# Attention mixer of a decoder trunk: layer norm and conv branch one head pair earlier, output tiles opened during the last scores

## The chip, the cores and the metric

The kernel runs on one core of a Trainium2 chip. The core has a matrix engine (PE; its weight loads are listed apart as PEld), a vector engine (DVE), a scalar engine for activation functions and copies (ACT), a general engine (POOL) and a queue engine (SP). Here POOL and SP are used mostly to start DMAs. Each engine works through its own list of instructions strictly in order, and a semaphore holds an instruction back until what it needs is there. The metric is the device time of one execution in microseconds (us), the median of several runs.

## What is computed

A trunk of two layers on 512 tokens of width 1024: a half-weighted SwiGLU block, a mixer, another half-weighted SwiGLU block, each on an RMS-normed input, and a last norm. The change is in the mixer of layer 0, which runs an attention branch and a convolution branch side by side:

```python
def hybrid_mixer(h, cos, sin, w_in, dw_w, dw_b, ln_g, ln_b, w_out):
    proj = h @ w_in
    q = apply_partial_rotary(heads(proj[..., :A_WIDTH]), cos, sin)
    k = apply_partial_rotary(heads(proj[..., A_WIDTH:2 * A_WIDTH]), cos, sin)
    v = heads(proj[..., 2 * A_WIDTH:3 * A_WIDTH])
    ...                      # three dilated windows of 8 heads, mixed by their softmax denominators
    u = proj[..., 3 * A_WIDTH:]
    glu = u[..., :CONV_CHANNELS] * jax.nn.sigmoid(u[..., CONV_CHANNELS:])
    c = causal_depthwise_conv(glu, dw_w) + dw_b
    c = jax.nn.silu(layer_norm(c, ln_g, ln_b))
    return jnp.concatenate([attn, c], axis=-1) @ w_out
```

The kernel folds the three windows into one softmax with an additive mask. All data are float32; a matrix product is made of three passes of the faster rounded format (high part by high part, low by high, high by low).

## The kernel before: how the mixer is staged

Data lie transposed: 128 channels on the partitions, 512 tokens along a row. The input of the output projection has eight chunks of 128 channels, `o_x[0..7]`. Chunks 0 to 3 are the four head pairs (two heads of 64 channels each), chunks 4 to 7 the four channel groups of the convolution branch. Each chunk is kept as a high part `hi` and a low part `lo`, made by `split` (ACT copy, L134, then DVE subtraction, L135).

`hybrid_heads` works head pair by head pair, `t` = 0 to 3:

- `raw_rows` projects q or k of a pair (24 matmuls, L140 to L142, of 128x512), and `rotate` applies the rotary part (a matmul with a permutation, L859; DVE L861, L862; then the high and low parts, ACT L864 and DVE L865, named `qh`, `ql`, `kh`, `kl`).
- `scores(t)` makes eight blocks of scores, four for each of the pair's two heads. A block is three matmuls (L880 to L882) of 128, 256, 384 or 512 columns into a PSUM tile named `sc`. DVE adds the mask and takes the row extreme (L885), ACT takes the exponential (L886). `normed` divides by the denominators (DVE L890, ACT L892).
- `values(t, b)` transposes a head's probabilities (ten transposes, L912), copies them out of PSUM (ACT L915, tiles `pt`) and multiplies by v (four float32 matmuls, L920) into a tile `po`. The values of pair t stand after the projections of pair t+1.

The convolution is a row of 31 DVE instructions per channel group (`taps`, L773 and L777). `layer_norm` is a Python generator in five steps, each started by a `next(ln)`: the sum over the four groups and the mean by a matmul (L925 to L928); subtraction of the mean, squares and their sum by matmuls (L932 to L941); the reciprocal root (L944 and `rsqrt`, ten small DVE instructions); its broadcast by matmuls (`row_bcast`, L156) and the multiplication (L951 to L953); Silu and `split` (L956, L957). In the kernel before, three of these steps stand before the scores of pair 3 and two behind them.

The output projection makes eight tiles d = 0 to 7 of 128 channels, each of 8 chunks times 3 matmuls (`out_mm`). Tiles 0 to 2 are begun in `hybrid_heads` with chunks 0, 1, 2 and completed in `hybrid` with chunks 4 to 7 and 3. Tiles 3 to 7 follow whole. The weights of one tile come in by `load_split`: a DMA from SP into a buffer `raw` (four buffers), an ACT copy into `whi` (L126), a second ACT copy with the sign turned into `wlo` (L127), and a DMA from POOL that adds the original onto it (L128). `whi` and `wlo` have three buffers each (`NWB`, L31), so the weights of tile 3 go into those of tile 0. `raw` of tile 3 is loaded long before.

PSUM has eight banks, in four groups of two: `mm`, `sc`, `po`, `tr`. The mean of the layer norm takes one of the two `sc` banks until the four subtractions L932 have read it. The order in which `hybrid` and `hybrid_heads` write their instructions is only a priority: a scheduler places them on the engines, and what it makes of them is read from the order of the built program.

Of the kernel before, what the change touches and what calls it, by code (L numbers as in the profile page):

```python
# [50 lines left out]
def trunk(ctx, tc, io, out, phases):  # L51
# [45 lines left out]
    def psum(tag):  # L97
        return pp.tile([P, T], F32, tag=tag, name=nm(tag))
# [614 lines left out]
    def hybrid(xn, nxt, ahead, take):  # L713
        with tc.tile_pool(name="ho", bufs=1, side="right", reuse_waits="tile") as op:
            with tc.tile_pool(name="hy", bufs=1, side="right", reuse_waits="tile") as hp:
                o_x, ps = hybrid_heads(xn, op, hp, take)
            xn.close()
            nxt.open()
            for d in range(NK):
                if d < 3:  # L720
                    out_mm(ps[d], take(20 + d), o_x, (4, 5, 6, 7, 3), False, True)
                else:
                    ps[d] = psum("po" if d % 2 else "mm")
                    wt = take(20 + d)
                    for _ in range((0, 0, 0, 0, 0, 0, 1, 1)[d]):
                        step(ahead)
                    out_mm(ps[d], wt, o_x, range(NK), True, True)
                V.tensor_add(h[d], ps[d], h[d])
                nxt.feed(d)
                for _ in range((0, 0, 0, 0, 0, 0, 2, 2)[d]):  # L730
                    step(ahead)
            nxt.fed()

    def out_mm(ps, wt, xs, ks, first, last):
        for k in ks:
            hi, lo = wt[k // 4]
            c = slice(k % 4 * P, k % 4 * P + P)
            mm3(ps, hi[:, c], lo[:, c], xs[k], first and k == ks[0], last and k == ks[-1])

    def hybrid_heads(xn, op, hp, take):  # L740
# [21 lines left out]
        pads, cv, o_x = [], [], [None] * NK  # L762
# [20 lines left out]
        def taps(n):  # L783
            for _ in range(n):
                next(conv, None)
# [61 lines left out]
        def raw_rows(i, n):  # L847
            ps = project(i)
            taps(n)
            qa = ht("qa", 2)  # L850
            A.activation(qa, ps, AF.Copy)
            u = ht("u", 2)
            V.tensor_mul(u, ps, Ct)
            return qa, u
# [10 lines left out]
            V.tensor_sub(lo, u, hi.bitcast(F32))  # L865
            return hi, lo

        def scores(t, q, k):
            qh, ql = q
            kh, kl = k  # L870
            probs = {}
            den = {b: ht("den", 4, n=4) for b in range(2)}
            rd = {b: ht("rd", 4, n=4) for b in range(2)}

            def score(b, i):
                rows = slice(64 * b, 64 * b + 64)
                w = (i + 1) * P
                c = slice(i * P, w)
                ps = psum("sc")
                PE.matmul(ps[:, :w], qh[rows, c], kh[rows, :w], start=True, stop=False)  # L880
                PE.matmul(ps[:, :w], qh[rows, c], kl[rows, :w], start=False, stop=False)
                PE.matmul(ps[:, :w], ql[rows, c], kh[rows, :w], start=False, stop=True)  # L882
                s = ht(f"s{i}", 2, n=w)
                m = ht("m", 8, n=1)
                V.tensor_tensor_reduce(s, ps[:, :w], K["mask"][:, T - w:], -0.125, 3.0e38, ALU.add, ALU.min, m)  # L885
                A.activation(s, s, AF.Exp, scale=-1.0, bias=m, accum_out=den[b][:, i:i + 1])  # L886
                probs[b, i] = s

            def normed(b):
                V.reciprocal(rd[b], den[b])  # L890
                for i in range(NT):
                    A.activation(probs[b, i], probs[b, i], AF.Copy, scale=rd[b][:, i:i + 1])  # L892

            for i in range(NT):
                score(0, i)
            score(1, 0)
            score(1, 1)
            normed(0)
            score(1, 2)
            score(1, 3)  # L900
            normed(1)
            return probs

# [18 lines left out]
        def layer_norm():  # L922
            mu = psum("sc")
            tot = ht("t1", 1)
            V.tensor_add(tot, cv[0], cv[1])  # L925
            V.tensor_add(tot, tot, cv[2])
            V.tensor_add(tot, tot, cv[3])
            PE.matmul(mu, K["o512"].to_broadcast([P, P]), tot, start=True, stop=True)  # L928
            yield
            acc = ht("t1", 1)  # L930
            for t in range(4):
                V.tensor_sub(cv[t], cv[t], mu)  # L932
                if t == 0:
                    A.activation(acc, cv[t], AF.Square)
                else:
                    sq = ht("qa", 2)
                    A.activation(sq, cv[t], AF.Square)
                    V.tensor_add(acc, acc, sq)
            st = psum("tr")
            for c in range(NT):  # L940
                PE.matmul(st[:, c:c + 1], acc[:, c * P:(c + 1) * P], K["o512"], start=True, stop=True)  # L941
            yield
            v = small(4, "nv")
            V.tensor_scalar(v, st[:, :4], EPS, None, op0=ALU.add)  # L944
            rl = rsqrt(v, 4, "rcol")
            yield
            rb = psum("tr")
            for c in range(NT):
                row_bcast(rl[:, c:c + 1], rb[:, c * P:(c + 1) * P])
            Rl = ht("t1", 1)  # L950
            A.activation(Rl, rb, AF.Copy)  # L951
            for t in range(4):
                V.tensor_mul(cv[t], cv[t], Rl)  # L953
            yield
            for t in range(4):
                A.activation(cv[t], cv[t], AF.Silu, scale=pr["lng"][:, t:t + 1], bias=pr["lnb"][:, t:t + 1])  # L956
                o_x[4 + t] = split(cv[t], op, "ox", 16)  # L957

        ln = layer_norm()
        q = raw_rows(12, 0)  # L960
        k = raw_rows(13, 4)
        qr = rotate(q, "q", 2)
        held = None
        out_ps = {}
        for t in range(NT):
            if t < 3:
                q = raw_rows(14 + 2 * t, 8)
            else:
                next(ln)
            kr = rotate(k, "k", 1)  # L970
            if held:
                values(t - 1, 0, *held)
            if t < 3:
                k = raw_rows(15 + 2 * t, 8)
                qn = rotate(q, "q", 2)
            else:
                next(ln)
            if held:
                values(t - 1, 1, *held)
                o_x[t - 1] = split(held[1], op, "ox", 16)  # L980
            if t == 3:
                next(ln)
            probs = scores(t, qr, kr)
            taps(5)
            qr = qn
            held = probs, psum("po")
        next(ln)
        for d in range(3):
            out_ps[d] = psum("sc" if d > 1 else "mm")
            out_mm(out_ps[d], take(20 + d, 3 - d), o_x, (0, 1, 2), True, False)  # L990
        next(ln, None)
        values(3, 0, *held)
        values(3, 1, *held)
        o_x[3] = split(held[1], op, "ox", 16)
# [458 lines left out]
```

## Time and profile before

| | |
|---|---|
| median of 3 runs | 2097.8 us (2097.16 to 2097.91) |
| the profiled execution | 2098.93 us, its span 2097.2 us |
| mean granted PE clock | 0.974 |
| busy share of the span | PE 96%, PEld 85%, DVE 77%, ACT 53%, POOL 6% |
| last output tile of the mixer complete (L728) | 621.98 us from the span's start |

Times within the profile are counted from the start of its span. A row of the timeline gives the start, the busy time, the engine, the line of the kernel and the operation, `output<-inputs` by the program's tile names with the buffer numbers left out, the shape, how many instructions were merged (x), and in square brackets how long the engine had been idle before and what ended that. A float32 matmul appears as two instructions. The busy time of a matmul covers its latency: what one costs in a row of others is the distance between two starts. PEclk is the granted clock as a share of the full one. In the table of windows, each engine has its busy time and the number of instructions in that stretch.

### The profile page before, as it was taken

What the parts mean: (1) busy time and instruction counts of PE and PEld (TensorE: products, weight loads), DVE (VectorE), ACT (ScalarE), POOL (GpSimd) and SP (SyncE); (2) the same over time, 40 slices, a digit from 0 to 9 for tenths busy, and PEclk for the clock granted to TensorE, in tenths of its full rate; (3) what the DMA queues carried; (4) which work ended last, traced back from release to release, by engine and by line L of the source; (5) the groups of instructions that cost most, each with busy time, mean ns of one, the idle gap of its engine ahead of it and who ended that gap; (6) DMA issues with size and microseconds to landing.
All of it is one profiled execution on the core that took longest, in us unless ns stands there. A gap on an engine that the chain in (4) does not pass through costs nothing.

```text
span 2097.2 us, 32970 instructions
## 1 busy us (share of the span) xinstructions
PE 2020.4 (96%) x12694; PEld 1785.7 (85%) x12694; DVE 1609.0 (77%) x2758; ACT 1113.9 (53%) x1981; POOL 134.0 (6%) x190
## 2 busy tenths in 40 slices
PE   7999999999999999998999999979989999999997
PEld 6999998786579999987999998767778878999986
DVE  5888879798567888889888788657585578888876
ACT  5444447547654444465444446676445654444455
POOL 0000000110000000000000000233302210000000
PEclk9999999999899999999999999999889999999998
DMA  3333332784143333322333332679635563333321
GB/s 125 101 103 109 101 100 83 183 194 97 29 101 116 101 104 108 96 86 84 107 104 105 101 101 82 183 215 231 137 106 131 121 132 107 109 101 102 104 87 46
DMA packets 108845, 237.70 MB, mean 113 GB/s; under 512 B 22160, under 2 KB 24976, under 8 KB 108688
## 3 DMA queue, kind: packets, MB, share of 16 engines
q1 hardware_dynamic: 90544, 193.06, 29.7%
q0 software_dynamic: 17616, 42.02, 10.8%
q8 instruction: 99, 1.62, 0.3%
q14 instruction: 58, 0.48, 0.1%
q10 hardware_dynamic: 528, 0.52, 0.1%
HBM read 224.55 MB, written 11.01 MB: 112 GB/s over the span
## 4 chain that ended last, share of the span: by engine, by line
PE 80%; DVE 8%; issue 5%; ACT 3%; DMA 3%; SPq 0%; POOL 0%; DVEq 0%; ACTq 0%; POOLq 0%
PE mm L141 13%; PE mm L140 13%; PE mm L142 13%; PE sc L141 7%; PE sc L140 7%; PE sc L142 7%; PE po L142 3%; PE po L141 2%; PE po L140 2%; PE tr L140 2%; PE tr L142 2%; PE tr L141 2%; DVE wlo L117 1%; DVE gl L386 1%; PE tr L1051 1%
## 5 line engine op out<-in xcount | busy, mean ns | idle before, releaser
L117 DVE TENSOR_TENSOR wlo<-raw,whi 128x1024 fp32r<-128x1024 f32 (+1 forms) x400 | 473.3, 1201 | 158.8 <-ACT whi L116 154.3
L140 PE MATMUL mm<-xh,whi 128*128 128x256 f32 (+2 forms) x1800 | 562.0, 312 | 8.7 <-ACT b L456 4.0
L142 PE MATMUL mm<-xh,wlo 128*128 128x256 f32 (+2 forms) x1800 | 557.9, 310 | 3.0 <-DMA wlo<-in_wgdn 3.0
L141 PE MATMUL mm<-xl,whi 128*128 128x256 f32 (+2 forms) x1800 | 556.3, 309 | 0.0
L116 ACT ACTIVATE whi<-raw 128x1024 fp32r<-128x1024 f32 (+1 forms) x400 | 404.8, 1034 | 33.9 <-issue 14.4
L140 PEld LDWEIGHTS mm<-xh,whi 128*128 128x128 f32 (+1 forms) x1800 | 344.7, 192 | 42.4 <-ACT b L456 7.2
L141 PEld LDWEIGHTS mm<-xl,whi 128*128 128x128 f32 (+1 forms) x1800 | 344.6, 191 | 26.3 <-issue 1.1
L142 PEld LDWEIGHTS mm<-xh,wlo 128*128 128x128 f32 (+1 forms) x1800 | 344.7, 192 | 20.5 <-DMA wlo<-in_wgdn 3.6
L140 PE MATMUL sc<-xh,whi 128*128 128x256 f32 x1056 | 299.8, 284 | 5.8 <-ACT xh L250 3.0
L141 PE MATMUL sc<-xl,whi 128*128 128x256 f32 x1056 | 299.0, 283 | 3.4 <-DVE xl L251 3.4
L142 PE MATMUL sc<-xh,wlo 128*128 128x256 f32 x1056 | 298.8, 283 | 0.9 <-DVE wlo L117 0.8
L140 PEld LDWEIGHTS sc<-xh,whi 128*128 128x128 f32 x1056 | 202.0, 191 | 7.8 <-ACT xh L250 3.6
L141 PEld LDWEIGHTS sc<-xl,whi 128*128 128x128 f32 x1056 | 202.1, 191 | 4.0 <-DVE xl L251 4.0
L142 PEld LDWEIGHTS sc<-xh,wlo 128*128 128x128 f32 x1056 | 202.1, 191 | 1.8 <-DVE wlo L117 1.8
L386 DVE TENSOR_TENSOR gl<-g,gh 128x512 fp32r<-128x512 f32 (+1 forms) x286 | 178.6, 643 | 32.3 <-ACT gh L385 30.0
L385 ACT ACTIVATE gh<-g 128x512 fp32r<-128x512 f32 (+1 forms) x286 | 166.4, 592 | 67.1 <-PE mm L141 34.8
L403 ACT ACTIVATE a<-a 128x512 f32<-128x512 f32 x88 | 55.6, 632 | 253.8 <-DVE a L402 253.8
L126 ACT ACTIVATE whi<-raw 128x512 fp32r<-128x512 f32 (+2 forms) x109 | 77.0, 734 | 97.9 <-PE mm L141 72.0
L442 ACT ACTIVATE b<-mm 128x256 f32<-128x256 f32 x84 | 32.2, 383 | 155.9 <-PE mm L142 155.9
L456 ACT ACTIVATE b<-mm 128x256 f32<-128x256 f32 x88 | 33.7, 383 | 141.0 <-PE mm L142 141.0
L141 PE MATMUL mm<-gl,whi 128*128 128x512 f32 (+1 forms) x220 | 83.1, 378 | 4.9 <-DVE gl L386 4.7
L777 DVE SCALAR_TENSOR_TENSOR cv<-pad,prm_t,cv 128x512 f32<-128x512 f32 x120 | 83.8, 743 | 0.8
(419 smaller groups left out, 3544.8 us busy)
## 6 DMA issues: line engine op xcount, KB each, us to landing
raw<-in_wf1i SPq DMA_DIRECT2D x82, 512.0 KB, 3.6
raw<-in_wf2i SPq DMA_DIRECT2D x82, 512.0 KB, 3.5
raw<-in_wgdn SPq DMA_DIRECT2D x32, 512.0 KB, 5.2
wlo<-in_wgdn POOLq DMA_DIRECT2D x64, 256.0 KB, 6.1
raw<-in_wf2i SPq DMA_DIRECT2D x56, 256.0 KB, 2.6
raw<-in_wf1i SPq DMA_DIRECT2D x52, 256.0 KB, 2.6
raw<-in_wf1b SPq DMA_DIRECT2D x20, 512.0 KB, 3.5
raw<-in_wf2b SPq DMA_DIRECT2D x20, 512.0 KB, 3.5
```

The source lines that it names most:

```text
L116: A.activation(hi[:, s], src[:, s], AF.Copy)
L117: V.tensor_sub(lo[:, s], src[:, s], hi[:, s].bitcast(F32))
L126: A.activation(hi[:, s], raw[:, s], AF.Copy)
L140: PE.matmul(ps, whi, xhi, start=first, stop=False, skip_group_check=skip)
L141: PE.matmul(ps, whi, xlo, start=False, stop=False, skip_group_check=skip)
L142: PE.matmul(ps, wlo, xhi, start=False, stop=last, skip_group_check=skip)
L385: A.activation(hi, g[f][:, s], AF.Copy)
L386: V.tensor_sub(lo, g[f][:, s], hi.bitcast(F32))
L403: A.activation(cg[f], cg[f], AF.Silu)
L442: A.activation(b0[f][:, HT:], pb[f][:, :HT], AF.Copy)
L456: A.activation(b1[f][:, :HT], pb[f][:, :HT], AF.Copy)
L777: V.scalar_tensor_tensor(acc, x, w, acc, op0=ALU.mult, op1=ALU.add)
```

## The change

Four things are written in another order; no arithmetic is changed, and no instruction is added to PE or DVE.

- The taps of the convolution are requested earlier: 10, 10 and 6 of them at each of pairs 0 and 1, then 8 and 3, in place of 8, 8 and 5 at every pair, so that none is left for pair 3.
- `layer_norm` begins one pair earlier: its first step stands before the scores of pair 2, the second behind them, the other three before the scores of pair 3.
- A generator `open_out` emits one piece behind each of the eight score blocks of pair 3: chunks 0, 1, then 4 to 7, then 2, for output tiles 0 and 1.
- Output tile 2 is emitted whole but for chunk 3 behind the scores. `hybrid` then adds only chunk 3 to tiles 0 to 2.

```diff
-                    out_mm(ps[d], take(20 + d), o_x, (4, 5, 6, 7, 3), False, True)
+                    out_mm(ps[d], take(20 + d), o_x, (3,), False, True)
...
-        def scores(t, q, k):
+        def scores(t, q, k, fill=lambda: None):
...
             for i in range(NT):
                 score(0, i)
+                fill()
             score(1, 0)
+            fill()
             score(1, 1)
+            fill()
             normed(0)
             score(1, 2)
+            fill()
             score(1, 3)
+            fill()
             normed(1)
...
+        def open_out():
+            for d, ks in ((0, (0, 1)), (1, (0, 1)), (0, (4, 5)), (1, (4, 5)), (0, (6, 7)), (1, (6, 7)),
+                          (0, (2,)), (1, (2,))):
+                if d not in out_ps:
+                    out_ps[d] = psum("mm")
+                out_mm(out_ps[d], take(20 + d, 3 - d), o_x, ks, ks[0] == 0, False)
+                yield
+
...
+        opening = open_out()
+        more = ((10, 10, 6), (10, 10, 6), (8, 3, 0))
         for t in range(NT):
             if t < 3:
-                q = raw_rows(14 + 2 * t, 8)
-            else:
+                q = raw_rows(14 + 2 * t, more[t][0])
+            kr = rotate(k, "k", 1)
+            if t == 3:
                 next(ln)
-            kr = rotate(k, "k", 1)
             if held:
                 values(t - 1, 0, *held)
             if t < 3:
-                k = raw_rows(15 + 2 * t, 8)
+                k = raw_rows(15 + 2 * t, more[t][1])
                 qn = rotate(q, "q", 2)
             else:
                 next(ln)
             if held:
                 values(t - 1, 1, *held)
                 o_x[t - 1] = split(held[1], op, "ox", 16)
+            if t == 2:
+                next(ln)
             if t == 3:
+                next(ln, None)
+            probs = scores(t, qr, kr, (lambda: next(opening, None)) if t == 3 else (lambda: None))
+            if t < 3:
+                taps(more[t][2])
+            if t == 2:
                 next(ln)
-            probs = scores(t, qr, kr)
-            taps(5)
             qr = qn
             held = probs, psum("po")
-        next(ln)
-        for d in range(3):
-            out_ps[d] = psum("sc" if d > 1 else "mm")
-            out_mm(out_ps[d], take(20 + d, 3 - d), o_x, (0, 1, 2), True, False)
-        next(ln, None)
+        out_ps[2] = psum("sc")
+        out_mm(out_ps[2], take(22, 1), o_x, (0, 1, 4, 5, 6, 7, 2), True, False)
         values(3, 0, *held)
         values(3, 1, *held)
         o_x[3] = split(held[1], op, "ox", 16)
```

What the scheduler makes of it, at three places. Lines behind the change are shifted: its L917, L925 and L933 are the L912, L920 and L928 of before. The first place is PE where the two programs part, while the values of pair 1 are still being made (`tr` and `po` tiles); before, the scores of pair 2 (`sc`) begin there:

```order
L880 MATMUL sc_5262<-kh_5151,qh_4987 128x128
L881 MATMUL sc_5262<-kl_5152,qh_4987 128x128
L912 MATMUL tr_5238<-cst,s_848_5066 128x128
L912 MATMUL tr_5238<-cst,s_851_5079 128x128
L912 MATMUL tr_5238<-cst,s_854_5087 128x128 x2
L882 MATMUL sc_5262<-kh_5151,ql_4988 128x128
```

With the change, output tiles 0 and 1 (`mm_5483`, `mm_5505`) are begun there with chunks 0 (`hi_5023`) and 1 (`hi_5258`, and `lo` beside them), and these rows lead up to the mean of the layer norm and the first score of pair 2:

```order
L140 MATMUL mm_5483<-hi_5258,whi_5114 128x512
L140 MATMUL mm_5505<-hi_5258,whi_5190 128x512
L141 MATMUL mm_5483<-lo_5259,whi_5114 128x512
L142 MATMUL mm_5483<-hi_5258,wlo_5115 128x512
L141 MATMUL mm_5505<-lo_5259,whi_5190 128x512
L933 MATMUL sc_5262<-t_892_5263,hcst 128x512
L880 MATMUL sc_5272<-kh_5161,qh_4996 128x128
L881 MATMUL sc_5272<-kl_5162,qh_4996 128x128
```

The pieces with chunks 0 and 1, written behind the scores of pair 3, have moved ahead of those of pair 2, and the scores of pair 2 stand behind the split of pair 1 and the mean. On PE and DVE every row ahead of this place is the same in both programs, the taps among them.

The second place is DVE between the last score block of pair 2 and the first of pair 3. Before, the low part of pair 3's k (`kl_5353`) came straight after the subtraction of the mean:

```order
L862 TENSOR_TENSOR u_5220<-u_5220,t_923_5349 128x512
L890 RECIPROCAL rd_5261<-den_5259 128x4
L932 TENSOR_TENSOR cv_4456<-cv_4456,sc_5341 128x512
L932 TENSOR_TENSOR cv_4702<-cv_4702,sc_5341 128x512
L932 TENSOR_TENSOR cv_4971<-cv_4971,sc_5341 128x512
L865 TENSOR_TENSOR kl_5353<-u_5220,kh_5352 128x512
```

With the change, it stands behind the last score block of pair 2 (`sc_5333`) and the small instructions of the reciprocal root:

```order
L885 ISA s_919_5337,m_5338<-sc_5333,hcst 128x512
L885 ISA m_5338 128x1
L862 TENSOR_TENSOR u_5224<-u_5224,t_928_5369 128x512
L150 TENSOR_TENSOR nt_5379<-rcol_5378 128x4
L151 SCALAR_TENSOR_TENSOR nt_5379<-nt_5379,nv_5376 128x4
L152 SCALAR_TENSOR_TENSOR rcol_5378<-nt_5379,rcol_5378 128x4
L150 TENSOR_TENSOR nt_5379<-rcol_5378 128x4
L151 SCALAR_TENSOR_TENSOR nt_5379<-nt_5379,nv_5376 128x4
L152 SCALAR_TENSOR_TENSOR rcol_5378<-nt_5379,rcol_5378 128x4
L150 TENSOR_TENSOR nt_5379<-rcol_5378 128x4
L890 RECIPROCAL rd_5271<-den_5269 128x4
...
L865 TENSOR_TENSOR kl_5373<-u_5224,kh_5372 128x512
```

The root has moved ahead of the scores of pair 3, and `kl`, for which those scores wait, behind most of it.

The third place is PE around the last values. Between the last score of pair 3 and the first transpose for its values, the change has 51 matmuls of output tiles 0 to 2 in one block, with no score among them. Then come the values, and these rows (`hi_5669` and `lo_5670` are chunk 3, the last one to be ready; `whi_5696` and `whi_5717` are the weights of tiles 3 and 4):

```order
L925 MATMUL po_5600<-pt_5658,vt_4583 64x128
L140 MATMUL mm_5483<-hi_5669,whi_5114 128x512
L140 MATMUL mm_5505<-hi_5669,whi_5190 128x512
L140 MATMUL sc_5601<-hi_5669,whi_5486 128x512
L141 MATMUL mm_5483<-lo_5670,whi_5114 128x512
L142 MATMUL mm_5483<-hi_5669,wlo_5115 128x512
L141 MATMUL mm_5505<-lo_5670,whi_5190 128x512
L142 MATMUL mm_5505<-hi_5669,wlo_5191 128x512
L141 MATMUL sc_5601<-lo_5670,whi_5486 128x512
L142 MATMUL sc_5601<-hi_5669,wlo_5487 128x512
L140 MATMUL po_5736<-hi_5023,whi_5696 128x512
L141 MATMUL po_5736<-lo_5024,whi_5696 128x512
```

Before, the same place had the rest of three tiles, 36 matmuls from the last of the values to the first of tile 3; it began so (`hi_5633` is chunk 3, `hi_5568` and `hi_5573` are chunks 4 and 5):

```order
L140 MATMUL mm_5530<-hi_5583,whi_5104 128x512
L141 MATMUL mm_5530<-lo_5584,whi_5104 128x512
L142 MATMUL mm_5530<-hi_5583,wlo_5105 128x512
L140 MATMUL mm_5547<-hi_5568,whi_5180 128x512
L140 MATMUL mm_5530<-hi_5633,whi_5104 128x512
L141 MATMUL mm_5547<-lo_5569,whi_5180 128x512
L142 MATMUL mm_5547<-hi_5568,wlo_5181 128x512
L141 MATMUL mm_5530<-lo_5634,whi_5104 128x512
L142 MATMUL mm_5530<-hi_5633,wlo_5105 128x512
```

27 matmuls have moved from behind the values of pair 3 to before them; nine are left there. On ACT the change has two more loads of a function table: Silu stands between the exponentials of pair 3, and the next block's first Silu (L403) loads its table again.

## Prediction

> **What bounds the kernel now.** I read the page's first two parts, then the timeline of PE, ACT and DVE around the last two head pairs, then a table of windows there.
>
> ```profile
> PE 2020.4 (96%) x12694; PEld 1785.7 (85%) x12694; DVE 1609.0 (77%) x2758; ACT 1113.9 (53%) x1981; POOL 134.0 (6%) x190
> PEclk9999999999899999999999999999889999999998
> 527.83:545.50 17.67, 16.94 (x70) 9.06 (x69) 12.34 (x33) 13.33 (x35) 0.87 (x1) 1.00 0.27 61
> 545.50:584.70 39.20, 36.78 (x125) 21.31 (x126) 13.78 (x42) 22.77 (x50) 0.00 (x0) 0.74 0.00 1
> 584.70:621.98 37.28, 36.26 (x157) 28.89 (x156) 28.05 (x47) 21.83 (x27) 4.32 (x5) 1.00 0.58 127
> ```
>
> PE sets the time nearly everywhere. In the page's eleventh digit the clock falls, and the windows (PE, PEld, DVE, ACT, POOL busy, then the clock) put it between 545.50 and 584.70. The windows are the three stages of my sum. The first begins where the two orders part, and ends with the first score of pair 3:
>
> ```profile
> 527.83 0.32 PE L880 MATMUL sc<-kh,qh 64*128 64x128 f32 x1
> 545.49 0.49 PE L880 MATMUL sc<-kh,qh 64*128 64x128 f32 x2 [0.73 <-ACT kh L864]
> 584.10 0.60 ACT L134 ACTIVATE hi<-po 128x512 fp32r<-128x512 f32 x1 [2.97 <-PE po L920]
> 585.73 0.40 PE L141 MATMUL mm<-lo,whi 128*128 128x512 f32 x1
> 586.17 1.06 ACT L126 ACTIVATE whi<-raw 128x1024 fp32r<-128x1024 f32 x1 [1.47 <-PE mm L141]
> 587.66 1.04 ACT L127 ACTIVATE wlo<-whi 128x1024 fp32r<-128x1024 f32 x1
> 589.00 0.86 POOL L128 DMA_DIRECT2D wlo<-in_whybo  x1 [58.93 <-ACT wlo L127]
> 594.14 0.50 PE L142 MATMUL po<-hi,wlo 128*128 128x512 f32 x1 [1.02 <-DMA wlo<-in_whybo]
> ```
>
> The second ends with chunk 3 (584.10 + 0.60 = 584.70). The third has the wait on which this change turns. Tile 0 ends with chunk 3. Only when PE has read its weights for the last time (585.73 + 0.40) may ACT copy tile 3's weights into the same buffer (586.17), and their low part is there at 594.14, 8.41 after that matmul began. Before, PE had tiles 1 and 2 to work on, and still waited 1.02.
>
> **First stage: pair 2's scores.** The taps do not move on any engine; the earlier requests cost and bring nothing. What moves is the mean, ahead of the scores. The prices:
>
> ```profile
> 521.07 2.37 PE L920 MATMUL po<-pt,vt 128*64 128x512 f32 x8
> 501.09 0.60 PE L912 MATMUL tr<-cst,s 128*128 128x128 f32 x4
> 588.30 0.39 PE L140 MATMUL mm<-hi,whi 128*128 128x512 f32 x1
> 588.53 0.40 PE L141 MATMUL mm<-lo,whi 128*128 128x512 f32 x1
> 500.23 1.02 PE L859 MATMUL tr<-qa,hcst 128*128 128x512 f32 x2
> L885 DVE CUSTOM_DVE_ANT_0 s<-sc,hcst x32: 280/486/692, 481.3 to 563.0; 128x128 f32<-128x128 f32 x8, 128x256 f32<-128x256 f32 x8, 128x384 f32<-128x384 f32 x8, 128x512 f32<-128x512 f32 x8
> L932 DVE TENSOR_TENSOR cv<-cv,sc x4: 656/679/682, 541.6 to 544.1; 128x512 f32<-128x512 f32 x4
> 551.67 0.16 DVE L150 TENSOR_TENSOR nt<-rcol 128x4 f32<-128x4 f32 x1
> 551.87 0.16 DVE L151 SCALAR_TENSOR_TENSOR nt<-nt,nv 128x4 f32<-128x4 f32 x1
> ```
>
> One projection matmul is 0.23 from start to start. From 527.83, five of them (1.2), six transposes (0.9), the four L920 (2.3) and switches between them (0.6) end pair 1's values at 532.8, a little earlier than before. Its split (0.60 on ACT, 0.69 on DVE with hand-offs) and the last matmuls of tiles 0 and 1 lead to 535.1. The mean, two float32 passes like L859, takes 0.86, and DVE sees it at 536.1.
>
> Then DVE carries pair 2's eight blocks together with the layer norm: L885 twice 0.28, 0.42, 0.56, 0.69 and the eight reads of 0.08 (4.5), four L932 and three L938 at 0.61 from start to start (4.3), rotary and small ones (1.5): 10.3 of work. The mean holds one of the two `sc` banks, so each early block waits for DVE to read the one before, and ahead of the last block PE has the sums of squares (about 1.0 to 1.2, L941 below) and an L859 (0.86, at half clock 1.7), 2.7 together. Following the rows hand to hand, I put the last block's reduction at 550.1, 14.0 after the mean, so 3.7 of waiting. Bounds: 10.3 if PE is always ahead, and 18.2, which before's pair 3 took for its eight blocks (545.49 to 563.7) with values between. I take 14.0, nearer to the work.
>
> Behind it on DVE stand L862 (0.6), nine or ten small instructions at 0.20 (2.0) and `kl` (0.69). So pair 3's scores begin at 553.5, not 545.5: **+8.0**. Queued behind the waiting DVE are `rd` and so pair 2's normalization; PE has nothing that does not wait for these.
>
> **The clock there.** The gate's own rows:
>
> ```profile
> 543.53:546.94 3.41, 2.68 (x12) 1.26 (x11) 2.06 (x5) 3.41 (x8) 0.00 (x0) 1.00 0.00 0
> 546.94:550.36 3.42, 2.96 (x17) 2.02 (x17) 2.77 (x9) 2.56 (x8) 0.00 (x0) 1.00 0.00 0
> 550.36:553.77 3.41, 3.41 (x15) 2.51 (x15) 1.34 (x7) 1.27 (x4) 0.00 (x0) 0.50 0.00 0
> 564.01:567.44 3.43, 3.43 (x13) 2.95 (x13) 1.35 (x4) 3.43 (x10) 0.00 (x0) 0.50 0.00 0
> 567.44:570.84 3.40, 3.09 (x18) 2.40 (x16) 1.65 (x3) 3.37 (x5) 0.00 (x0) 1.00 0.00 0
> 574.24:577.68 3.44, 3.26 (x6) 1.03 (x6) 1.36 (x2) 1.69 (x4) 0.00 (x0) 0.50 0.00 0
> 575.34 3.50 PE L920 MATMUL po<-pt,vt 128*64 128x512 f32 x8
> ```
>
> The clock is 1.00 or 0.50, and changes at the ends of stretches of 3.4. It fell at 550.36 behind a stretch that held little but small scores, without an idle gap over 0.73. With the change, 536 to 550 is such a stretch four times over, and emptier, so I expect half clock from about 540. It came back at 577.68 behind a stretch of transposes and L920; with the change the first such stretch is 557 to 560.6. [...]
>
> **Second stage: to chunk 3.** More prices, the scores between two switches, the mean squares and the broadcast at half clock, and ACT's:
>
> ```profile
> 510.28 0.33 PE L880 MATMUL sc<-kh,qh 64*128 64x128 f32 x1
> 511.16 0.50 PE L140 MATMUL mm<-xh,whi 128*128 128x512 f32 x1
> 507.05 0.44 PE L880 MATMUL sc<-kh,qh 64*128 64x384 f32 x1
> 508.46 0.50 PE L142 MATMUL mm<-xh,wlo 128*128 128x512 f32 x1
> 549.57 1.18 PE L941 MATMUL tr<-hcst,t 128*128 128x1 f32 x8
> 563.52 1.91 PE L156 MATMUL tr<-cst,rcol 128*128 128x128 f32 x8
> 538.55 1.90 ACT L892 ACTIVATE s<-s,rd 128x128 f32<-128x128 f32 x4
> L956 ACT ACTIVATE cv<-cv,prm_t x4: 798/800/816, 569.7 to 572.9; 128x512 f32<-128x512 f32 x4
> ```
>
> From 553.5 PE always has work:
>
> - pair 3's scores, 0.88 + 1.41 a head, less two L880 done ahead: 4.3
> - values: 1.5 for ten transposes and 2.3 for L920; three heads whole and one without eight transposes: 14.0
> - broadcast of the root: 0.8
> - block of 51 matmuls at 0.233: 11.9
> - last split and hand-off: 0.7
>
> That is 31.7 at full clock. Half clock from 553.5 to 560.6 adds 3.55, short waits for `pt` and `hi` 0.6. Chunk 3 is ready at 553.5 + 35.9 = 589.4, against 584.70. ACT's own chain stands beside the block. Pair 2's values end at 567.0 (9.9 of the list above, and the 3.55). Then ACT has three Silu (2.1), five splits (2.5), the table (1.3), five exponentials (3.2), two normalizations (3.7) and a hand-off (0.3): 580.1. The block of 51 follows pair 3's last score at 568.9 and ends at 581.3 with its waits for `lo`, so ACT is covered by 1.2 and takes over beyond that. The stage shrinks by 3.3 (39.2 to 35.9), the first grew by 8.0: **+4.7** in all.
>
> **Third stage: the output tiles.** 27 matmuls fewer stand here, 27 × 0.233 = 6.3, and one would book that as the gain. It cannot be had: the chain from tile 0's last L141 to tile 3's low weights is not shortened. Before, that L141 began 1.03 after chunk 3; now it is behind three high-part matmuls, 0.80 after. The chain grows from 8.41 to 9.37, since ACT's order has tile 4's L126 (0.96 from start to start) ahead of tile 3's L127. Of what follows (594.14 to 621.98, 27.84), two more matmuls are done ahead, 0.47. 0.80 + 9.37 + 27.84 − 0.47 = 37.54 against 37.28: **+0.3**. PE stands idle some 6.4 in the middle, so the clock falls. It would come back 2.7 to 6.1 after PE resumes, by where the stretch falls; half of the mean is **+2.2** (1.4 to 3.0).
>
> **Behind the mixer.** The next block's first Silu loads its table again.
>
> ```profile
> L886 ACT ACT_TABLE_LOAD  x1: 1283/1283/1283, 482.1 to 482.1; - x1
> 641.88 0.63 ACT L403 ACTIVATE a<-a 128x512 f32<-128x512 f32 x1 [0.76 <-DVE a L402]
> 643.78 0.38 PE L140 MATMUL mm<-xh,whi 128*128 128x256 f32 x1 [0.43 <-ACT b L429]
> ```
>
> 1.28, of which 0.76 fits into the wait for DVE; PE waits for ACT two instructions on: **+0.5**.
>
> **Sum.** 4.7 + 0.3 + 2.2 + 0.5 = +7.7. The profiled execution took 2098.93, 1.13 above the median; the sum goes onto both, 2106.6 for a profiled one and **2105.5** for the median. A difference of 0.2%, 4.2 us, is about what a measurement of this kernel can tell from no change.
>
> **The rivals.**
>
> - *Clock holds through pair 2's scores* (0.15). The first stage is 3.0 shorter (L859 0.85 and half of the scores), the second 3.55: −1.85 at chunk 3, with the third stage +1.15. 2098.9, no change. For it: two stretches below full load kept the clock, as 543.53 to 546.94. Against: the stretch after it.
> - *The weights do not gate* (0.08). If tile 3's weights were there as soon as PE comes to them, the 6.3 would be a gain, and the clock would not fall: with the held clock −1.85 − 6.3 + 0.5, 2090.2. That needs the chain to be under 2.1, and 594.14 shows 8.41.
> - *Half clock goes on into the block of 51* (0.17). Pair 3's last scores wait for DVE between them; if the stretch from 567 counts as idle, the block runs at half clock for 3.4 and ACT's late table loads come out of cover: +3 to +6 more, 2109 to 2112.
> - My case has 0.60; its own range is 2101 to 2109, from the bounds of the 14.0 that the rows make likely (±2.5) and of the clock terms (±1.5).
>
> The range of 2097.5 to 2112 takes in the held clock and the longer half clock. Faster 0.12 (the third case, and DVE at its bound with everything else good), no change 0.18, slower 0.70.
>
> **What would show it.** In the profile of the changed kernel: the first score of pair 3 near 553 and the clock at 0.50 before it; chunk 3's split near 589; a gap of PE of about 6 at tile 3's first L142, released by the DMA of `wlo`, with the clock at 0.50 behind it; ACT's table load ahead of L403. I am wrong in the first stage if pair 3's scores begin before 549, in the second if PE waits for ACT ahead of the last transposes, in the third if PE's gap at tile 3 is under 3.

## The result and the profile after

The change makes the kernel slower: 2106.06 us (median of 7, 2102.28 to 2114.3) against 2097.16 (7 runs, 2095.07 to 2097.91), a ratio of 1.0047 with a 95% interval of 1.003 to 1.0063. The forecast was 2105.5. The profiled execution of the change took 2102.28, where 2106.6 had been forecast for a profiled one.

In the table of windows of the changed kernel the three stages of the sum are cut at the same work as before. They are longer by 5.5, shorter by 1.6 and longer by 2.3:

```profile
526.13:549.30 23.17, 19.89 (x71) 11.76 (x69) 15.14 (x41) 13.07 (x32) 0.87 (x1) 0.80 0.20 46
549.30:586.93 37.63, 35.74 (x147) 22.76 (x147) 11.33 (x34) 25.14 (x53) 0.00 (x0) 0.90 0.00 1
586.93:626.53 39.60, 33.19 (x131) 25.69 (x132) 27.50 (x47) 21.63 (x27) 4.32 (x5) 0.91 0.55 120
```

Its timeline, at the places named in the prediction:

```profile
533.28 1.02 PE L933 MATMUL sc<-t,hcst 128*128 128x512 f32 x2
534.34 1.28 DVE L937 TENSOR_TENSOR cv<-cv,sc 128x512 f32<-128x512 f32 x2 [1.32 <-PE sc L933]
...
547.18 0.69 DVE L885 CUSTOM_DVE_ANT_0 s<-sc,hcst 128x512 f32<-128x512 f32 x1 [0.81 <-PE sc L882]
547.80 0.69 DVE L862 TENSOR_TENSOR u<-u,t 128x512 f32<-128x512 f32 x1
549.30 0.79 PE L880 MATMUL sc<-kh,qh 64*128 64x128 f32 x2 [0.26 <-ACT kh L864]
550.05 0.68 DVE L865 TENSOR_TENSOR kl<-u,kh 128x512 fp32r<-128x512 f32 x1
550.79 0.47 PE L881 MATMUL sc<-kl,qh 64*128 64x128 f32 x1 [0.69 <-DVE kl L865]
...
586.33 0.60 ACT L134 ACTIVATE hi<-po 128x512 fp32r<-128x512 f32 x1 [1.91 <-PE po L925]
587.79 0.42 PE L141 MATMUL mm<-lo,whi 128*128 128x512 f32 x1
597.19 0.79 PE L142 MATMUL po<-hi,wlo 128*128 128x512 f32 x1 [6.15 <-DMA wlo<-in_whybo]
626.53 0.69 DVE L728 TENSOR_TENSOR h<-po,h 128x512 f32<-128x512 f32 x1 [0.46 <-PE po L142]
647.11 1.28 ACT L403 ACT_TABLE_LOAD   x1
648.41 0.63 ACT L403 ACTIVATE a<-a 128x512 f32<-128x512 f32 x1
```

All four signs that the prediction named are there: pair 3's scores late (549.30 against 545.49), chunk 3 at 586.33 + 0.60 = 586.93 against 584.70, a gap of 6.15 ahead of tile 3's first L142, ended by the DMA of `wlo`, and the table load ahead of L403. The first of them came late by less than forecast: 549.30 is only 0.3 past the 549 before which the prediction would have called its first stage wrong. The clock, in windows of 3.41 counted from where it changes:

```profile
536.71:540.12 3.41, 1.95 (x10) 1.44 (x11) 3.41 (x12) 2.62 (x7) 0.00 (x0) 1.00 0.00 0
540.12:543.53 3.41, 3.41 (x15) 2.97 (x15) 1.72 (x8) 3.17 (x10) 0.00 (x0) 0.50 0.00 0
553.77:557.19 3.42, 3.42 (x6) 1.05 (x6) 0.57 (x2) 1.47 (x5) 0.00 (x0) 0.50 0.00 0
557.19:560.60 3.41, 3.41 (x24) 2.59 (x22) 0.83 (x2) 1.09 (x2) 0.00 (x0) 1.00 0.00 0
591.32:594.73 3.41, 0.00 (x0) 0.00 (x0) 3.41 (x7) 3.41 (x5) 0.86 (x1) 1.00 0.79 197
594.73:598.15 3.42, 0.96 (x2) 0.83 (x3) 2.40 (x4) 3.07 (x5) 0.92 (x2) 0.50 1.00 172
598.15:601.56 3.41, 3.41 (x9) 2.64 (x8) 0.00 (x0) 0.00 (x0) 0.81 (x1) 0.50 1.04 240
```

It fell at 540.12, behind a stretch of ten small score matmuls in which PE was busy 1.95 of 3.41, and came back at 557.19. The second fall, at 594.73, stands behind a stretch without a single matmul, within the gap of 6.15. Ahead of the first there was no such gap: none between the mean and 540.12 was over 0.73.

This profile is the fastest of the seven executions, and its span is only 3.0 above that of before (2100.2 and 2097.2). The stretch described next is 6.2 longer, but what stands ahead of it took 1.7 less and what stands behind it 1.5 less. So the whole is compared by medians, and the mechanism over one stretch, **M**: from the second matmul of the rotary step of pair 3's q (L859, some 1.0 ahead of the place where the two orders part) to the start of the last L728. In this profile of the change it is 101.35, in that of before 95.11, with PE idle 11.6 and 4.2 of it (length less PE's busy time):

```profile
525.18:626.53 101.35, 89.77 (x354) 60.86 (x353) 54.29 (x121) 60.78 (x113) 5.19 (x6) 0.88 0.26 58
```

```profile
526.87:621.98 95.11, 90.95 (x354) 59.76 (x353) 54.49 (x121) 58.90 (x112) 5.18 (x6) 0.89 0.28 62
```

The expectations below call the start of M the rotary matmul of pair 3's k; it is that of its q.

### The profile page after: what moved, and what is told of

Read it like the earlier page. It is cut to its first block, busy times and chain, and to the rows that moved or that the text cites. A ratio compares the mean times of both kernels' runs of the same rounds, so it can differ in the third digit from the quotient of the medians.

```text
span 2100.2 us, 32971 instructions
## 1 busy us (share of the span) xinstructions
PE 2016.1 (96%) x12694; PEld 1784.2 (85%) x12694; DVE 1610.3 (77%) x2758; ACT 1117.0 (53%) x1983; POOL 133.8 (6%) x190
## 4 chain that ended last, share of the span: by engine, by line
PE 81%; DVE 8%; issue 5%; ACT 3%; DMA 2%; SPq 0%; POOL 0%; DVEq 0%; ACTq 0%; POOLq 0%
PE mm L141 13%; PE mm L140 13%; PE mm L142 13%; PE sc L141 7%; PE sc L140 7%; PE sc L142 7%; PE po L142 3%; PE po L140 2%; PE po L141 2%; PE tr L140 2%; PE tr L142 2%; PE tr L141 2%; PE tr L1068 1%; DVE wlo L117 1%; DVE gl L386 1%
## 5 line engine op out<-in xcount | busy, mean ns | idle before, releaser
L142 PE MATMUL mm<-xh,wlo 128*128 128x256 f32 (+2 forms) x1800 | 557.1, 310 | 3.1 <-DMA wlo<-in_wgdn 3.1
L142 PEld LDWEIGHTS mm<-xh,wlo 128*128 128x128 f32 (+1 forms) x1800 | 343.8, 191 | 20.8 <-DMA wlo<-in_wgdn 3.8
L142 PE MATMUL sc<-xh,wlo 128*128 128x256 f32 x1056 | 299.4, 284 | 1.3 <-DVE wlo L117 1.2
L142 PEld LDWEIGHTS sc<-xh,wlo 128*128 128x128 f32 x1056 | 202.7, 192 | 2.2 <-DVE wlo L117 2.2
L403 ACT ACTIVATE a<-a 128x512 f32<-128x512 f32 x88 | 55.6, 632 | 253.1 <-DVE a L402 253.1
```

The source lines that it names most:

```text
L142: PE.matmul(ps, wlo, xhi, start=False, stop=last, skip_group_check=skip)
L403: A.activation(cg[f], cg[f], AF.Silu)
```

## The experiments

My theory (A) was that of the prediction: the mean and the half clock ahead of pair 3's scores, then tile 3's weights. The rivals were the moment at which the stretches of half clock fall, ACT, and a DVE that sets the pace whatever the clock. Each M comes from a single execution, and before's two differ by 1.9, so a smaller difference between two rows shows nothing by itself. "Fill" stands for unused matmuls between score blocks.

| kernel | M | whole, median of n | before, same chip, median | ratio, 95% |
|---|---|---|---|---|
| the change again | 101.17 | 2106.23 of 5 | 2095.88 | 1.0038 to 1.0063 |
| layer norm alone | 101.10 | 2105.49 of 5 | 2095.88 | 1.0037 to 1.0061 |
| output tiles alone | 100.58 | 2104.96 of 5 | 2095.88 | 1.0031 to 1.0055 |
| tile 3's own buffers | 97.99 | 2101.47 of 12 | 2095.88 | 1.0019 to 1.0041 |
| before again | 93.23 | 2094.84, one run | 2097.61 | |
| mean in `po` | 101.60 | 2106.28 of 6 | 2097.61 | 1.0036 to 1.0063 |
| tile 2 late | 98.00 | 2103.92 of 6 | 2097.61 | 1.0026 to 1.0057 |
| fill, pair 2 | 97.37 | 2099.01 of 12 | 2097.61 | 1.0003 to 1.0029 |
| fill and tile 2 late | 92.89 | 2096.60 of 12 | 2097.51 | 0.998 to 1.0008 |
| fill in before | 96.86 | 2097.72 of 12 | 2097.51 | 0.9988 to 1.0015 |
| layer norm back and tile 2 late | 97.74 | 2100.82 of 12 | 2098.23 | 1.0001 to 1.0025 |
| half the fill and tile 2 late | 99.51 | 2099.05 of 12 | 2097.63 | 0.999 to 1.0017 |

**Both kernels again.** Unaltered, for a second profile of each.

> The changed kernel once more, unaltered, for a second profiled execution and five more times. Theory A (the price lies in the mixer: pair 2's scores behind the mean, and the reload of tile 3's weights): about 2106, the second profile shows the PE gap ahead of tile 3's first L142 again at 5.5 to 6.5, half clock from about 540 to 557 and again behind the gap, and the last L728 comes 99 to 103 after the place where the two orders part. Theory B (most of the 8.9 is the moment at which the clock gate's stretches happen to fall): the gap is there, but the half clock begins and ends elsewhere, and the times spread over 8 or more again.

> The kernel before once more, unaltered, for a second profiled execution. In its first profile the clock was at 0.50 for 17.1 around pair 3's scores; where only output tiles were moved, the same scores in the same order had 6.8. Theory A (the gate's 3.4-us stretches stand at another place in every execution, and decide in the kernel before how long that half clock lasts): from the rotary matmul of pair 3's k to the last L728 it takes 95.1 with 17 of half clock and 90 to 93 with 7. Theory B (the half clock belongs to the order of the work): 17.1 of it and 95 again, within 0.5.

The windows of M, of the change and then of before, with the stretch from pair 3's first score to chunk 3 (39.20 at clock 0.74 in before's first profile) as a second row:

```profile
527.09:628.26 101.17, 89.17 (x354) 60.61 (x353) 54.32 (x121) 60.79 (x113) 5.19 (x6) 0.88 0.27 58
```

```profile
525.58:618.81 93.23, 86.42 (x354) 56.66 (x353) 54.40 (x122) 58.88 (x112) 5.18 (x6) 0.95 0.30 63
544.19:581.06 36.87, 32.26 (x125) 18.22 (x126) 13.71 (x42) 22.77 (x50) 0.00 (x0) 0.86 0.00 1
```

The change repeats to 0.2. Before does not: it had about half the half clock (0.95 in place of 0.89) and M was 1.9 shorter, with the same instructions. So the second expectation's B (the half clock belongs to the order of the work) falls for before, and the profile I predicted from was one with much half clock. The change costs 6.1 to 8.1 in M.

**The two halves.** Layer norm alone (output tiles written as before), and output tiles alone:

```diff
 (layer norm alone, against the change)
-                    out_mm(ps[d], take(20 + d), o_x, (3,), False, True)
+                    out_mm(ps[d], take(20 + d), o_x, (4, 5, 6, 7, 3), False, True)
...
-            probs = scores(t, qr, kr, (lambda: next(opening, None)) if t == 3 else (lambda: None))
+            probs = scores(t, qr, kr, lambda: None)
...
-        out_ps[2] = psum("sc")
-        out_mm(out_ps[2], take(22, 1), o_x, (0, 1, 4, 5, 6, 7, 2), True, False)
+        for d in range(3):
+            out_ps[d] = psum("sc" if d > 1 else "mm")
+            out_mm(out_ps[d], take(20 + d, 3 - d), o_x, (0, 1, 2), True, False)
 (output tiles alone, against before)
-                    out_mm(ps[d], take(20 + d), o_x, (4, 5, 6, 7, 3), False, True)
+                    out_mm(ps[d], take(20 + d), o_x, (3,), False, True)
...
         next(ln, None)
+        for d in range(3):
+            out_mm(out_ps[d], take(20 + d, 1), o_x, (4, 5, 6, 7), False, False)
```

> Only the layer norm and the taps are moved; output tiles 0 to 2 are written as before (chunks 0 to 2 behind pair 3's scores, chunks 4 to 7 and 3 in the output projection). The order of the built program shows that the scheduler puts their chunks 4 to 7 ahead of chunk 3 by itself, since the layer norm's outputs are ready by then: nine matmuls are left behind chunk 3, as in the full change. Theory A: so this part alone makes nearly the whole difference, 2105 (2102 to 2108), with PE's gap at tile 3's first L142 at 5.5 to 6.5. Rival (the pieces written between pair 3's scores are what costs): near the kernel before, 2098.

> Layer norm and taps stand as before; only chunks 4 to 7 of output tiles 0 to 2 are written ahead of pair 3's values, so nine matmuls are left behind chunk 3. Theory A: pair 3's scores begin as before, near 545.5; the 27 matmuls that stood behind chunk 3 now stand ahead of it, so chunk 3 comes some 5 later than before's 584.7, and behind it PE waits 5.5 to 6.5 for tile 3's low weights and loses 2 to 3 of clock: 2104 to 2107. Rival (the late scores of pair 3 are the whole price, and the weights no matter): within 1 of the kernel before, 2097 to 2098.

Each half makes the whole loss, as expected. The rows of M and of the gap at tile 3, of the layer norm and then of the tiles:

```profile
526.36:627.46 101.10, 90.49 (x354) 60.17 (x353) 54.18 (x122) 60.54 (x113) 5.18 (x6) 0.88 0.27 58
```

```profile
598.41 0.79 PE L142 MATMUL po<-hi,wlo 128*128 128x512 f32 x1 [6.30 <-DMA wlo<-in_whybo]
```

```profile
569.11 0.50 PE L140 MATMUL mm<-hi,whi 128*128 128x512 f32 x1 [3.79 <-ACT hi L134]
597.69 0.80 PE L142 MATMUL po<-hi,wlo 128*128 128x512 f32 x1 [6.34 <-DMA wlo<-in_whybo]
```

With an early layer norm the scheduler moves chunks 4 to 7 ahead by itself, so the pieces between pair 3's scores cost nothing of their own. Without it, PE waits 3.79 for Silu's `hi` in front of the moved matmuls and 6.34 for tile 3's weights behind them.

**The weights of tile 3.** In buffers of their own, and with tile 2 made behind tiles 0 and 1 to cover the reload:

```diff
 (own buffers, against the change; ... stands for lines left out)
...
+        w3 = [(ht("pad", 4, F32R, 30 + T)[:, :T], ht("pad", 4, F32R, 30 + T)[:, :T]) for _ in range(2)]
+        take(23, 1, w3)
         values(3, 0, *held)
...
+        for d in range(3):
+            out_mm(out_ps[d], take(20 + d, 1), o_x, (3,), False, True)
+        out_ps[3] = psum("po")
+        out_mm(out_ps[3], take(23, 1), o_x, range(NK), True, True)
 (tile 2 late, against the change)
-                if d < 3:
+                if d < 2:
                     out_mm(ps[d], take(20 + d), o_x, (3,), False, True)
...
-        out_ps[2] = psum("sc")
-        out_mm(out_ps[2], take(22, 1), o_x, (0, 1, 4, 5, 6, 7, 2), True, False)
```

> The full change, but output tile 3's weights go into buffers of their own (the four padded rows of the convolution, dead by then), so their copies and DMAs run tens of us ahead and nothing of tile 0 is waited for. Theory A: PE's gap of 6 at tile 3's first L142 goes, the clock stays at 1.00 behind it, and the last L728 comes 8 to 9 earlier than with the change: 2097 to 2098, level with the kernel before, since the 27 matmuls done ahead now pay back what pair 3's late scores cost. Rival (the gap is filled by another wait, for tile 4's weights in tile 0's buffer): a gap of 3 or more at tile 4 and 2102 to 2104.

> The full change, but output tile 2 isn't begun ahead of the values of pair 3: it is made whole behind tiles 0 and 1, in the bank that tile 0 leaves. So 21 matmuls stand where PE waited for tile 3's low weights, and no buffer is added. Theory A: the gap at tile 3's first L142 falls from 6.2 to 6.5 to 1 to 2, the clock does not fall behind it, chunk 3 comes 1 earlier (ACT's chain, not the block of matmuls, is then ahead of pair 3's last transposes): 2101 to 2103. Rival (tile 2 waits for DVE's addition of tile 0 and the gap only moves): 2105 to 2106.

Own buffers took 3.3 from M, not 8: PE then waits for tile 4's weights, which now go into tile 0's buffers. The rival was nearer: 2.59 at tile 4 and 2101.5. With tile 2 late the gap is 1.68, ACT holds up two transposes of pair 3's values by 1.04, and M is 3.3 shorter. Up to pair 3's last score PE's order is that of the change, so the difference comes from where the output tiles stand. The median, 2103.92, is just above the 2101 to 2103 expected:

```profile
601.71 0.79 PE L142 MATMUL mm<-hi,wlo 128*128 128x512 f32 x1 [2.59 <-DMA wlo<-in_whybo]
```

```profile
580.53 0.44 PE L917 MATMUL tr<-cst,s 128*128 128x128 f32 x2 [1.04 <-ACT pt L920]
598.50 0.50 PE L142 MATMUL po<-hi,wlo 128*128 128x512 f32 x1 [1.68 <-DMA wlo<-in_whybo]
```

**The mean's bank.**

```diff
-            mu = psum("sc")
+            mu = psum("po")
```

> The full change, with the mean of the layer norm in a bank of the group po in place of sc, so that pair 2's scores have both sc banks. Theory A (the bank that the mean holds makes each early block of pair 2 wait for DVE): three or four of PE's waits of 0.4 to 0.74 ahead of these blocks go, pair 3's scores begin 1 to 2 earlier, 2104 to 2105. Rival (DVE's own work carries pair 2's scores, and PE only waits elsewhere): waits of the same sum, 2106 again.

Most of the waits between the blocks went, and nothing was gained (2106.28, as the rival had it):

```profile
546.84 0.98 PE L946 MATMUL tr<-hcst,t 128*128 128x1 f32 x4 [6.62 <-DVE t L943]
```

The scheduler put four score blocks ahead of the mean, and PE then waited 6.62 in one piece for the squares, ahead of L946. The rotary matmul of pair 3's k (L859) stands behind L946 in PE's order. So this isn't a test of the bank alone. In this order, too, it is the layer norm's chain that holds pair 3's k.

**The half clock.** Seven float32 matmuls whose result is not used, each started by a block's row extreme `m`:

```diff
...
                 probs[b, i] = s
+                if wps is not None:
+                    if ms:
+                        PE.matmul(wps[:, :HT], ms[-1].to_broadcast([P, P]), K["mask"][:, :HT], start=True, stop=True)
+                    ms.append(m)
...
```

> The full change with seven float32 matmuls of 128x256 added between pair 2's score blocks, their result unused: 0.43 each at full clock, 3.0 in all, of which some 2.3 fit into PE's waits there. Theory A (half clock through pair 2's scores is a large part of the price): the clock holds at 1.00 or falls much later than at 540, pair 3's scores begin 1 to 2 earlier, chunk 3 comes 3 to 5 earlier, 2101 to 2103. Rival (DVE sets the pace there and the clock costs nothing): nothing gained and 0.5 to 3 lost, 2106 to 2109.

The clock held until tile 3's gap (6.64, up to 593.24). Pair 3's scores begin 22.5 after the start of M (24.1 with the change), chunk 3 is ready 56.7 after it (61.8), though PE has seven more matmuls to do. The median is 2099.01, below the 2101 to 2103 expected; by medians the fill took off 7.5 to 9, about twice what M shows in this execution, and where the rest lies is open. M, and the rows of these places:

```profile
525.84:623.21 97.37, 87.90 (x368) 59.45 (x367) 54.15 (x121) 60.94 (x113) 5.19 (x6) 0.95 0.28 60
```

```profile
548.33 0.49 PE L880 MATMUL sc<-kh,qh 64*128 64x128 f32 x2
```

```profile
581.91 0.60 ACT L134 ACTIVATE hi<-po 128x512 fp32r<-128x512 f32 x1 [1.91 <-PE po L929]
```

The fill is not the only difference. The rotary matmul of pair 3's k (L859) now stands ahead of the last two score blocks of pair 2, and with the change it stood behind the block of 384 columns. Two rows with the fill, then two of the change:

```profile
543.15 1.10 PE L859 MATMUL tr<-qa,hcst 128*128 128x512 f32 x2
544.62 0.44 PE L880 MATMUL sc<-kh,qh 64*128 64x384 f32 x1
```

```profile
540.70 0.52 PE L880 MATMUL sc<-kh,qh 64*128 64x384 f32 x1
543.51 2.06 PE L859 MATMUL tr<-qa,hcst 128*128 128x512 f32 x2
```

So the gain belongs to the clock and to another order together, and how it divides is not shown. The one comparison of a clock alone is that of before's two profiles: M was 1.9 shorter with about half as much half clock.

> The seven unused matmuls between pair 2's scores and the late output tile 2, together, on the full change. Apart they took 3.9 and 3.3 from the 101.3 between the rotary matmul of pair 3's k and the last L728. Theory A (the two prices, half clock and tile 3's weights, are separate): 94 there, and with the next block's table load 7 to 8 under the change, level with the kernel before within 1.5. Rival (the gains overlap: with a shorter block of matmuls ACT's normalization of pair 3 is last ahead of the transposes): 96 to 97, 2 to 3 above the kernel before.

With both cures the clock is 1.00 throughout M, and M is 0.3 below before's better draw. Together they took 8.4 from M, apart 3.9 and 3.3: the gains do not overlap, and together they make up the whole loss there. The kernel is level with before; it isn't faster by anything that can be measured.

```profile
525.97:618.86 92.89, 85.98 (x368) 57.40 (x367) 54.53 (x121) 61.09 (x113) 5.18 (x6) 1.00 0.30 63
```

> The kernel before, with the same seven unused matmuls between the score blocks of pair 3. Its two profiles had 20.5 and 10.2 of half clock there, and 95.1 and 93.2 from the rotary matmul to the last L728. Theory A (that half clock costs it, too): the clock holds until the last score of pair 3, 91 to 92.5, the whole 1 to 3 below the kernel before. Rival (PE then waits for ACT's Silu ahead of chunk 4's matmuls, 3.8 in the second profile, and the gain is lost there): level with the kernel before within 1.

The time is the rival's (level with before within 1), but neither theory describes the profile: the clock fell at 547.79 all the same. The stretch ahead of the fall has PE busy 2.38, and the first of the unused matmuls stands behind it, at 547.80:

```profile
544.38:547.79 3.41, 2.38 (x12) 1.28 (x10) 2.06 (x6) 3.17 (x7) 0.00 (x0) 1.00 0.00 0
547.79:551.21 3.42, 3.41 (x7) 1.81 (x7) 2.07 (x6) 1.70 (x6) 0.00 (x0) 0.50 0.00 0
```

> As the two together (unused matmuls between pair 2's scores, late output tile 2), with the seven unused matmuls at half their size, 128x128, 0.21 each by the larger ones. Theory A (the clock holds there as long as a stretch isn't mostly small scores and waits, and half the fill is enough): the clock still 1.00 from 530 to 570, 92 to 93 from the rotary matmul of pair 3's k to the last L728, the whole level with the kernel before. Rival (the fill has to be near its size): the clock falls at 540 to 545, 95 to 97, some 2 to 3 above the kernel before.

In its profile the clock fell to 0.50 at 540.37, the rival's place, and M is 99.51, above the 95 to 97 that the rival gave; the median is 1.4 above before's, level with it by the interval. But the edit did more than halve the fill: all eight score blocks of pair 2 now stand ahead of the rotary matmul of pair 3's k, and pair 3's first score comes 29.8 after the start of M (22.5 with the larger fill):

```profile
550.21 2.05 PE L859 MATMUL tr<-qa,hcst 128*128 128x512 f32 x2
556.40 0.49 PE L880 MATMUL sc<-kh,qh 64*128 64x128 f32 x2 [1.02 <-ACT kh L864]
```

So it does not tell how much fill is enough.

**The layer norm's place.** Against tile 2 late, its steps as in before up to the root:

```diff
-            kr = rotate(k, "k", 1)
-            if t == 3:
+            else:
                 next(ln)
+            kr = rotate(k, "k", 1)
...
-            if t == 2:
-                next(ln)
             if t == 3:
+                next(ln)
+                next(ln)
                 next(ln, None)
...
-            if t == 2:
-                next(ln)
```

> As with the late output tile 2, but the layer norm's steps stand where the kernel before has them, up to the root (mean ahead of pair 3's rotation, squares and root between pair 2's values); broadcast, Silu and the pieces of output tiles 0 and 1 stay ahead of and between pair 3's scores. So pair 2's scores have both banks and PE again has values to make beside the layer norm. Theory A (the place of the mean, ahead of pair 2's scores, is what delays pair 3 and drops the clock): pair 3's first score 18.5 to 19 after its rotary matmul instead of 24.1, the mixer from there to the last L728 at 92 to 94 against 98.0, the whole level with the kernel before within 2, with a half clock in pair 3's scores of 7 to 17 by execution. Rival (Silu and its two table loads between pair 3's exponentials hold PE ahead of pair 3's values): 96 to 98, some 3 above the kernel before.

Pair 3's first score is back at 18.6 after the start of M, but the profile has half clock from there for most of the way to chunk 3 (0.71), and M is only 0.3 under tile 2 late. PE also waits 2.45 for Silu's `hi`. M and the median are the rival's (96 to 98, some 3 above before); how much of it is Silu and how much the clock, this run does not separate:

```profile
544.60 0.49 PE L880 MATMUL sc<-kh,qh 64*128 64x128 f32 x2 [0.72 <-ACT kh L864]
569.18 1.22 PE L140 MATMUL mm<-hi,whi 128*128 128x512 f32 x2 [2.45 <-ACT hi L134]
```

```profile
544.60:585.59 40.99, 36.84 (x128) 22.72 (x128) 13.79 (x42) 24.39 (x51) 0.00 (x0) 0.71 0.00 1
```

The medians say more than this one profile: 2.6 above before, where tile 2 late is 6.3. So the layer norm's place costs some 3.7 by medians; the two intervals, 1.0001 to 1.0025 and 1.0026 to 1.0057, only just part. In this execution the early first score brought next to nothing, since the clock then fell.

## Why the prediction was right

- *First stage, +8.0: measured +5.5.* The mean reaches DVE 8.2 after the parting (8.3 forecast), and DVE is done with pair 2's last reduction 13.5 later, at 547.80 (14.0). The step that failed is the last: "So pair 3's scores begin at 553.5", which put all of them behind `kl`. The first L880 needs only `kh`, from ACT, and begins 1.5 behind that reduction, not 3.4. `kl` is ready 2.9 behind it (3.3 forecast) and holds the L881, at 550.79.
- *The clock.* Half from 540.12 to 557.19, one stretch less than forecast. With the fill, and the order that it brought, M is 3.9 shorter (101.3 less 97.4), net of what the fill itself takes. The first rival, a held clock, had been put at 2098.9; the fill, with which it held, measured 2099.01.
- *Second stage, −3.3: measured −1.6.* PE had 1.9 of waits in place of 0.6, and half clock, from 549.30 to 557.19, took 3.9 (half of these 7.89) in place of 3.55. Chunk 3 came 2.2 later by the profile's clock and 3.9 from the parting (+4.7 forecast). ACT was covered, as forecast.
- *Third stage, +0.3 and +2.2 of clock: measured +2.3.* The chain took 587.79 to 597.19, 9.40, against 9.37. The clock came back at 601.56, 4.37 after PE resumed, where the estimate was 2.7 to 6.1. The 27 matmuls done ahead came back as the gap; tile 2 late and own buffers confirm it, each by 3.3 of M.
- *Behind the mixer, +0.5: measured 2.0 by before's first profile, 0.8 by its second.* From the last L728 to L403's activation before again took 639.94 − 618.81 = 21.1, the first profile 19.9, the change 21.9. Its second profile took 21.6, so the price lies between 0.5 and 2.0. The row of before again:

```profile
639.94 0.63 ACT L403 ACTIVATE a<-a 128x512 f32<-128x512 f32 x1 [0.76 <-DVE a L402]
```

Sum: 5.5 − 1.6 + 2.3 + 2.0 = 8.2 against the first profile of before (7.7 forecast); 8.1 + 0.8 = 8.9 against the second. The medians differ by 8.9 here and by 10.35 in the repeat. So the mechanism was right: late scores under half clock, and a reload that moved matmuls do not shorten. That the sum came so close is partly luck. Against before's first profile the forecast was 2.5 too long in the first stage, 1.7 too short in the second, 0.2 too long in the third and 1.5 too short behind the mixer, and these nearly cancel. What the forecast lacked was the draw: the same instructions of before take 93.2 or 95.1.

## What to carry to other kernels

Before moving work ahead of a wait, ask when the buffers that feed what follows come free: here the next weights hung on the last read of the first tile's buffers, and 6.3 of moved matmuls became 6 of idle PE. Look at the granted clock behind stretches of small matmuls that wait for each other: here it was 0.50 from 540.12 on, and with seven unused matmuls between them it stayed at 1.00 (536.40 to 546.60), with another order beside it, and M was 3.9 shorter. Compare stretches that hold the change, over more than one execution, rather than two spans.

## What the hardware showed beside that

- Within M, in the first profiles of before and of the change, the clock was 1.00 or 0.50, and half clock lasted whole numbers of stretches of 3.41 (before: five from 550.36 and one from 574.24; the change: five from 540.12 and two from 594.73). How much of the work it took in differed by execution: the two profiles of before had mean clocks of 0.89 and 0.95 in M, over the same instructions.
- The time differs by execution far from the change, too. From the last L728 to the end of the span, which holds the same work in all kernels but for a table load, the profiles took 1473.6 (change), 1478.3 (again), 1475.2 (before) and 1474.3 (again), at mean clocks of 0.98, 0.97, 0.97 and 0.98. How much of that is the clock was not worked out.
- In before, half clock began behind a stretch with PE busy 2.96 of 3.42 (546.94), and full clock went on behind one with 2.68 of 3.41 (543.53). So busy time in the stretch ahead did not decide alone. Both had small scores; what else counts stays open.
